# Neighbourhood attention in a transformer block: two tiles for the side transposes, other steps for the splits of the output weights, and other places for the first output sums

## The chip, the cores and the metric

The kernel runs on one core of a Trainium2 chip. The metric is the device time of one execution in microseconds (us), lower is better; a comparison uses the median of several runs. The engines are named as the profile names them: PE (TensorE, with PEld for its weight loads), DVE (VectorE), ACT (ScalarE), POOL (GpSimd) and SP (SyncE, which issues most transfers).

## The reference, cut to what matters

One layer of a trunk on 1024 latent tokens (a grid of 16 rows by 64 columns) and 256 context tokens, width 1024. The part that the change touches is the attention of 8 heads of 64 and the output projection behind it:

```python
def row_block(r):                      # one row of the grid, clamped window of 8 x 16 keys
    ...
    s_loc = jnp.einsum('bnqhd,brnkhd->bhnqrk', q_r, k_b).astype(jnp.float32) * scale
    bias = rpb[:, dr_idx[None, None, :, None], dc_idx]
    s_loc = jnp.where(col_mask, s_loc + bias.astype(jnp.float32), -jnp.inf)
    s_ctx = jnp.einsum('bnqhd,bkhd->bhnqk', q_r, k_ctx).astype(jnp.float32) * scale
    s = jnp.concatenate([s_loc.reshape(B, H, NA_NCB, NA_QB, n_loc), s_ctx], axis=-1)
    p = jax.nn.softmax(s, axis=-1).astype(v.dtype)
    o = (jnp.einsum('bhnqrk,brnkhd->bnqhd', p_loc, v_b)
         + jnp.einsum('bhnqk,bkhd->bnqhd', p_ctx, v_ctx))
...
mix_x = jnp.concatenate([_pool_mixer(u_x, pool_w[l], pool_scale[l]), attn_x], axis=-1) @ w_out[l]
x = x + gt1 * _rmsnorm(mix_x, g_post_mix[l])
```

Before it stand norm, modulation and the projections to pooling input, queries, keys and values; behind it a squared-ReLU MLP of width 4096. All arrays are float32.

## The kernel before

**Precision.** Large products are made from split operands: a high part (a rounded copy, made on ACT) and a low part (source minus high part, made on DVE), and three matmuls hi·hi, hi·lo, lo·hi (`three`, L168 to L170).

**Stages.** Projections with 8 PSUM banks in one pool up to 236 us; attention and the first two output tiles, 236 to 369 us; the remaining output tiles, norm, and the MLP in 7 products per pair of blocks (a Strassen-like scheme) up to the end.

**Attention.** A unit `(j, m)` is a pair of heads j and a band m of 8 columns of the grid, 128 tokens; there are 4 x 8 = 32 units. Bands 1 to 6 are inner (640 keys: three bands and the context), bands 0 and 7 are edge units (512 keys). The loop over `i` (36 rounds) works on four units at once, each at another stage:

- `scores(i)`: four matmuls for two heads into two tiles `S` of two banks each (L665; pool `ps_s` holds 2 of them); then on DVE one instruction for each head that adds the bias table and keeps the row minimum `nm` (L679).
- `turn(i - 2)`: PE transposes (L707) of unit i-2. The shares (one over the sums, made by `share`) and, for an inner unit, the fifth block of the probabilities go to the "sides", columns 256 to 448 of each half of the tile `pa` (1024 columns, two banks); four blocks go to two banks `T` of pool `ps_t`.
- `fifth_kept(i - 2)`: one copy on ACT (L720) takes the sides of both halves to `px` in SBUF, 2 x 192 columns for an inner unit, 2 x 64 for an edge unit.
- `exps(i, e)`: exponential on ACT (L688), one for each head. Between them `turn_kept` copies the two banks `T` to `pt` (L725), the first on ACT, the second on DVE.
- `values(i - 3)`: 20 matmuls (16 for an edge unit) into columns 0 to 256 of `pa` (L740).
- `weighed(i - 4)`: DVE multiplies the result in `pa` by the shares, into `f` (L750).

`mixed_split` splits a finished half of a head pair (`f` to `mix`) in rounds 8, 15, 16, 23, 24, 31, 32; `weight_load` and `weight_split` bring and split the first half of the output weights in the rounds that `LOADS` and `HALVES` name. Of a split, `high` (L761) issues the ACT part at once and puts off the DVE part to the next call of `low` (L762), one round later.

In the last rounds, behind the value matmuls, `out_sums` makes the first output tile in the left half of a tile `po` of pool `ps_s`; after the loop `out_kept` reads it (on ACT the sum of squares, L130; on DVE the product with the gate, L800), and then the second output tile is made in the right half of `po`. The other six tiles of that half of the columns follow as `pw` in a new pool of 8 banks.

**Order.** Instructions of PE, ACT, DVE and SP stand in the order in which the code issues them (`in_order`). The framework adds the waits: it tracks who reads and writes a tile, and accesses of two engines to one tile of PSUM wait for each other; a pool that takes over memory waits for the tiles of the pool before. SBUF pages of 1024 columns come from one pool of 33, and a new one waits for the last user of the page that it gets.

Of the kernel before, what the change touches and what calls it, by code (L numbers as in the profile page):

```python
# [10 lines left out]
F32 = mybir.dt.float32  # L11
# [6 lines left out]
P = 128  # L18
# [7 lines left out]
HD = 64  # L26
# [53 lines left out]
def hybrid_block(ctx, tc, x, ctx_in, w_mod, b_mod, gp1, gp2, w_in, pool_w, rpb, w_out, w1, w2, vectors,  # L80
                 mask, edge, out):
    nc = tc.nc
# [12 lines left out]
    def sm(name, n, bufs=1):  # L95
        return small.tile([P, n], F32, tag=name.split("_")[0], name=name, bufs=bufs)

    def page(name, dt=F32):
        return act.tile([P, 1024], dt, tag="pg", name=name)
# [29 lines left out]
    def mean_square(junk, src, ms):  # L129
        nc.scalar.activation(junk, src, AF.Square, scale=D ** -0.5, accum_out=ms)  # L130
# [32 lines left out]
    def wk(w, k, lo, c, n):  # L163
        return w[k // 2][lo][:, (k % 2) * 512 + c : (k % 2) * 512 + c + n]


    def three(ps, ahi, alo, bhi, blo, first, last, more=False):
        nc.tensor.matmul(ps, ahi, bhi, start=first, stop=False, skip_group_check=more)  # L168
        nc.tensor.matmul(ps, ahi, blo, start=False, stop=False, skip_group_check=more)  # L169
        nc.tensor.matmul(ps, alo, bhi, start=False, stop=last, skip_group_check=more)  # L170
# [46 lines left out]
    with tc.tile_pool(name="ps1", bufs=8, space=PSUM) as ps1, tc.tile_pool(name="tmp1", bufs=3) as tmp:  # L217

        def bank(name):
            return ps1.tile([P, 512], F32, tag="mm", name=name)  # L220
# [413 lines left out]
    with (  # L634
# [8 lines left out]
        units = [(j, m) for j in range(4) for m in range(NM)]  # L643
        probs, least, sums, shares, turns, turned, fifths, mixed = {}, {}, {}, {}, {}, {}, {}, {}

        pa = ps_o.tile([P, 1024], F32, tag="pa", name="pa")
        sides = pa.rearrange("p (h f) -> p h f", h=2)[:, :, 256:448]


        def scores(i):  # L650
            j, m = units[i]
            inner = 0 < m < NM - 1
            n = NKEY if inner else 4 * P
            o = 1 if m == 0 else 0
            q = qT[j][m // 4]
            cols = slice((m % 4) * P, (m % 4 + 1) * P)
            heads = [slice(e * HD, (e + 1) * HD) for e in range(2)]
            S = [ps_s.tile([P, 1024], F32, tag="S", name=f"S{j}_{m}_{e}") for e in range(2)]
            if inner:
                parts = ((128, kT[j][:, (m - 1) * P : (m + 2) * P]), (512, kc[:, j, :]))  # L660
            else:
                parts = ((0, kc[:, j, :]), (256, kT[j][:, (m + o - 1) * P : (m + o + 1) * P]))
            for c0, keys in parts:
                for e, hs in enumerate(heads):
                    nc.tensor.matmul(S[e][:, c0 : c0 + keys.shape[1]], q[hs, cols], keys[hs], start=True, stop=True)  # L665
            halves = lambda a: a.rearrange("p (a b) -> p a b", a=2)
            for e in range(2):
                t = tabs[j % 2][e]
                sp = att.tile([P, NKEY], F32, tag="sp", name=f"sp{j}_{m}_{e}", bufs=6)[:, :n]
                if inner:  # L670
                    s, bt, to = S[e][:, 128:768], t[:, :NKEY], sp
                else:
                    s, to = halves(S[e][:, 0:512]), halves(sp)
                    if o:
                        bt = halves(t[:, 2 * P : 8 * P])[:, :, P:]
                    else:
                        bt = halves(t[:, NLOC : NLOC + 512])
                nm = sm(f"nm_{i}_{e}", 1, 6)
                nc.vector.tensor_tensor_reduce(out=to, in0=s, in1=bt, scale=1.0, scalar=BIG, op0=add, op1=ALU.min,  # L679
                                               accum_out=nm)  # L680
                probs[i, e] = sp
                least[i, e] = nm
# [16 lines left out]
        def turn(i):  # L699
            inner = 0 < units[i][1] < NM - 1  # L700
            t = [bank(f"T{i}_{h}") for h in range(2)]
            turned[i] = t
            halves = [slice(h * HD, (h + 1) * HD) for h in range(2)]

            def both(to, src):
                for h, hs in enumerate(halves):
                    nc.tensor.transpose(to(h), src(hs), ident[hs, hs])  # L707

            both(lambda h: sides[:, h, :HD], lambda hs: shares[i][hs])
            for e in range(2 if inner else 0):  # L710
                both(lambda h: sides[:, h, (e + 1) * HD : (e + 2) * HD], lambda hs: probs[i, e][hs, 4 * P : 5 * P])
            for c in range(4):
                for e in range(2):
                    o = (4 * e + c) * HD
                    both(lambda h: t[h][:, o : o + HD], lambda hs: probs[i, e][hs, c * P : (c + 1) * P])

        def fifth_kept(i):
            n = (3 if 0 < units[i][1] < NM - 1 else 1) * HD
            fifths[i] = att.tile([P, 384], F32, tag="px", name=f"px{i}", bufs=4).rearrange("p (h t) -> p h t", h=2)
            nc.scalar.copy(fifths[i][:, :, :n], sides[:, :, :n])  # L720

        def turn_kept(i, h, copy):
            if h == 0:
# [29 lines left out]
        N = len(units)  # L753

        kks = (2, 3, 0, 1)
        raw_o, wo = {}, {}
        LOADS, HALVES = (9, 14, 20, 24), (13, 17, 19, 21, 25, 27, 29, 30)
        lows = []

        def high(src, hi, lo):  # L760
# [3 lines left out]
        def low():  # L764
            while lows:
                lows.pop(0)()
# [12 lines left out]
        def weight_load(h, kk):  # L779
            raw_o[h, kk] = page(f"wor{h}_{kk}")  # L780
            nc.sync.dma_start(raw_o[h, kk].rearrange("p (a f) -> p a f", a=2), pair(w_out, kk, h * 512, 512))
# [6 lines left out]
        def out_sums(ps, w, t, ns):  # L788
            b, i = t // 4, t % 4
            for n in ns:  # L790
                k, mp = order[n], mix[b][order[n]]
                three(ps, mp[:, i * P : (i + 1) * P], mp[:, 512 + i * P : 512 + (i + 1) * P],
                      wk(w, k, 0, 0, 512), wk(w, k, 1, 0, 512), n == 0, n == 7)

        def out_kept(h, t, ps, jk):
            hs = slice(h * 512, (h + 1) * 512)
            if h == 0:
                mp1[t] = page(f"mp1_{t}")
            mean_square(jk, ps, ssm[h][:, t : t + 1])
            nc.vector.tensor_tensor(mp1[t][:, hs], ps, G1[:, hs], mul)  # L800

        with in_order(ET.PE, ET.Activation, ET.DVE, ET.SP):
            for i in range(N + 4):
                if i < N and units[i][1] == 2 and units[i][0] < 3:
                    tables(units[i][0] + 1)
                if i in LOADS:
                    weight_load(0, kks[LOADS.index(i)])
                if i == N - 2:
                    G1 = gate_page("a")
                if i > 3:  # L810
                    weighed(i - 4)
                low()
                if i > 8 and i % 8 == 7:
                    mixed_split(i // 8 - 1, 1)
                if i > 0 and i % 8 == 0:
                    mixed_split(i // 8 - 1, 0)
                if i in HALVES:
                    weight_split(HALVES.index(i))
                if i < N:
                    scores(i)  # L820
                if 1 < i <= N + 1:
                    turn(i - 2)
                    fifth_kept(i - 2)
                if i < N:
                    exps(i, 0)
                if 1 < i <= N + 1:
                    turn_kept(i - 2, 0, nc.scalar.copy)
                if i < N:
                    exps(i, 1)
                if 1 < i <= N + 1:  # L830
                    turn_kept(i - 2, 1, nc.vector.tensor_copy)
                if i < 2:
                    queries(2 + i, 1, bank(f"pq{2 + i}_1"), 0)
                if 0 < i <= N:
                    share(i - 1)
                if 2 < i <= N + 2:
                    values(i - 3)

                if i == N:
                    po = ps_s.tile([P, 1024], F32, tag="S", name="po")  # L840
                if i >= N:
                    out_sums(po[:, :512], wo, 0, ((0, 1), (2, 3, 4), (5, 6, 7), ())[i - N])
            out_kept(0, 0, po[:, :512], page("jo0_0")[:, :512])
            mixed_split(3, 1)
            low()
            out_sums(po[:, 512:], wo, 1, range(8))
            out_kept(0, 1, po[:, 512:], page("jo0_1")[:, :512])

    with tc.tile_pool(name="ps2", bufs=8, space=PSUM) as ps2:

# [3 lines left out]
      with ExitStack() as tmp2:  # L854
# [323 lines left out]
        with in_order(ET.PE) as first:  # L1178
            for p in range(0, EARLY, 2):
                both = [q for q in (p, p + 1) if q < EARLY]  # L1180
# [16 lines left out]
        with tc.issue_after(first[ET.PE]), in_order(ET.PE, ET.Activation, ET.DVE, ET.SP):  # L1197
# [10 lines left out]
            def halves(name):  # L1208
                both = [page(f"{name}{i}") for i in range(2)]
                return [both[t // 2][:, (t % 2) * 512 : (t % 2) * 512 + 512] for t in range(4)]  # L1210
# [131 lines left out]
```

## Time and profile before

| | |
|---|---|
| median of 3 runs | 1073.55 us (1073.38 to 1074.51) |
| the profiled execution | 1073.15 us, its span 1071.4 us |
| busy in the span | PE 1048.6 us, DVE 686.0, ACT 504.8, POOL 55.6 |
| mean granted PE clock | 0.997 |
| attention rounds 4 to 31 (first score matmul 256.52, end of round 31 at 347.98) | 91.46 us |
| first output tile ends, second begins, third begins | 359.9, 361.52, 368.78 us |

The span is the time from the first to the last instruction of the profiled execution. In the rows of the profile a line such as `L720 ACT COPY px<-pa 128x384` gives the source line, the engine, the operation, output and input tile (buffer numbers left out), and the shape; in a timeline the first two columns are start and duration, `xN` the number of instructions merged into the row, and the bracket tells how long the engine had been idle before and what ended that. In the table of waits the columns are the total, the number and the longest wait.

### The profile page before, as it was taken

The numbers are of one execution on the slowest core, as the hardware profiler recorded it, in microseconds if no ns is written. First come the engines' busy times: TensorE is split into PE (matmuls) and PEld (weight loads), VectorE is DVE, ScalarE is ACT, GpSimd is POOL, SyncE is SP. The second block draws the span as 40 slices with busy tenths as digits, with TensorE's granted clock in tenths as the row PEclk, the third lists the DMA queues.
The fourth block names the chain that finished last, engine by engine and source line by source line (L and its number), as shares of the span: only waits on it lengthen the run. The fifth ranks groups of instructions, "written<-read, shape, count | busy, mean of one in ns | idle before, by whom it ended". The sixth has DMA issues, their size and how long they took to land.

```text
span 1071.4 us, 15228 instructions
## 1 busy us (share of the span) xinstructions
PE 1048.6 (98%) x5873; PEld 857.9 (80%) x5873; DVE 686.0 (64%) x1072; ACT 504.8 (47%) x849; POOL 55.6 (5%) x109
## 2 busy tenths in 40 slices
PE   7999999999999899999999999999999999999996
PEld 6788888867777688878888888888888888888885
DVE  5536624845899225699887667664577667556586
ACT  6553120236888123776555555454454334334441
POOL 2020000030120002200000000000000000000001
PEclk9999999999999999999999999999999999999999
DMA  9905740431010603546753535445596765546556
GB/s 341 319 21 208 246 155 0 160 109 40 22 60 30 189 1 107 170 156 196 233 201 123 191 128 166 139 144 190 194 391 231 260 240 197 197 162 212 176 185 207
DMA packets 94268, 179.37 MB, mean 167 GB/s; under 512 B 6898, under 2 KB 39154, under 8 KB 94196
## 3 DMA queue, kind: packets, MB, share of 16 engines
q1 hardware_dynamic: 76644, 144.80, 40.9%
q10 hardware_dynamic: 16272, 29.40, 7.4%
q0 software_dynamic: 1280, 4.21, 1.1%
q8 instruction: 46, 0.75, 0.3%
q14 instruction: 26, 0.21, 0.1%
HBM read 140.62 MB, written 37.76 MB: 166 GB/s over the span
## 4 chain that ended last, share of the span: by engine, by line
PE 87%; ACT 5%; DVE 4%; issue 1%; DMA 1%; POOL 1%; SPq 0%; DVEq 0%; POOLq 0%; ACTq 0%
PE pk L374 4%; PE pyv L168 3%; PE pyz L168 3%; PE pyx L169 3%; PE pyx L168 3%; PE phz L170 3%; PE phv L170 3%; PE phv L169 3%; PE phz L169 3%; PE pyv L170 3%; PE pyz L170 3%; PE pyv L169 3%; PE pyz L169 3%; PE phv L168 3%; PE phz L168 3%; PE pyx L170 3%
## 5 line engine op out<-in xcount | busy, mean ns | idle before, releaser
L992 ACT ACTIVATE c<-c 128x512 f32<-128x512 f32 x48 | 30.3, 632 | 60.4 <-DVE c L1091 23.8
L688 ACT ACTIVATE sp<-sp,nm 128x640 f32<-128x640 f32 (+1 forms) x64 | 51.4, 803 | 11.6 <-DVE nm L679 11.0
L679 DVE CUSTOM_DVE_ANT_0 sp<-S,tab 128x640 f32<-128x640 f32 (+1 forms) x56 | 42.9, 802 | 18.5 <-PE S L665 11.9
L144 DVE TENSOR_TENSOR wpS<-S,wpS 128x512 fp32r<-128x512 f32 x64 | 43.6, 686 | 12.2 <-ACT wpS L143 12.2
L168 PE MATMUL phx<-thB,wpA 128*128 128x512 f32 x128 | 50.0, 391 | 0.9 <-ACT s L1050 0.9
L170 PE MATMUL phx<-thB,wpA 128*128 128x512 f32 x128 | 49.8, 389 | 0.0
L169 PE MATMUL phx<-tlB,wpA 128*128 128x512 f32 x128 | 49.8, 389 | 0.0
L143 ACT CAST wpS<-S 128x512 fp32r<-128x512 f32 x64 | 39.1, 616 | 18.0 <-PE phy L170 7.3
L139 POOL TENSOR_TENSOR ry<-vy,nhalf 128x1 f32<-128x1 f32 x8 | 4.4, 548 | 601.9 <-DVE vy L137 601.9
L993 ACT ACTIVATE c<-c 128x512 f32<-128x512 f32 x48 | 30.3, 632 | 9.9 <-DVE sa L1063 7.7
L1099 DVE TENSOR_TENSOR c<-phz,u 128x512 f32<-128x512 f32 x16 | 11.0, 690 | 32.1 <-PE phz L170 32.1
L168 PEld LDWEIGHTS phx<-thB,wpA 128*128 128x128 f32 x128 | 24.0, 188 | 6.3 <-ACT s L1050 1.3
L665 PE MATMUL S<-kT,q 64*128 64x384 f32 (+1 forms) x128 | 28.3, 495 | 0.4 <-DVE nm L679 0.4
L800 DVE TENSOR_TENSOR mp<-pw,Ga 128x512 f32<-128x512 f32 x14 | 9.6, 688 | 29.4 <-ACT jo L130 29.4
L740 PE MATMUL pa<-pt,v 128*64 128x128 f32 x352 | 25.9, 279 | 2.3 <-ACT px L720 1.1
L170 PEld LDWEIGHTS phx<-thB,wpA 128*128 128x128 f32 x128 | 24.0, 188 | 5.1 <-DVE wpA L144 0.2
L169 PEld LDWEIGHTS phx<-tlB,wpA 128*128 128x128 f32 x128 | 24.0, 188 | 5.0
L170 PE MATMUL phv<-thT,wpS 128*128 128x512 f32 x64 | 24.9, 389 | 0.0
L168 PE MATMUL phy<-thT,wpS 128*128 128x512 f32 x64 | 24.9, 389 | 0.0
L169 PE MATMUL phy<-tlT,wpS 128*128 128x512 f32 x64 | 24.9, 389 | 0.0
L170 PE MATMUL phy<-thT,wpS 128*128 128x512 f32 x64 | 24.9, 389 | 0.0
L168 PE MATMUL phz<-thT,wpS 128*128 128x512 f32 x64 | 24.9, 389 | 0.0
(919 smaller groups left out, 3242.8 us busy)
## 6 DMA issues: line engine op xcount, KB each, us to landing
b<-in_w SPq DMA_DIRECT2D x64, 512.0 KB, 4.5
hrS<-hdS SPq DMA_DIRECT2D x32, 512.0 KB, 4.7
hrA<-hdA SPq DMA_DIRECT2D x24, 512.0 KB, 5.1
wm<-in_w_mod SPq DMA_DIRECT2D x16, 512.0 KB, 9.9
wa_0w<-in_w SPq DMA_DIRECT2D x16, 512.0 KB, 5.1
wa_1w<-in_w SPq DMA_DIRECT2D x16, 512.0 KB, 4.3
hdA<-c ACTq DMA_DIRECT2D x32, 256.0 KB, 3.4
hdS<-sa ACTq DMA_DIRECT2D x32, 256.0 KB, 4.0
```

The source lines that it names most:

```text
L143: nc.scalar.copy(hi, src)
L144: nc.vector.tensor_tensor(lo, src, hi.bitcast(F32), sub)
L168: nc.tensor.matmul(ps, ahi, bhi, start=first, stop=False, skip_group_check=more)
L169: nc.tensor.matmul(ps, ahi, blo, start=False, stop=False, skip_group_check=more)
L170: nc.tensor.matmul(ps, alo, bhi, start=False, stop=last, skip_group_check=more)
L374: nc.tensor.matmul(pks[b][j], wk(wgt, k, low, j * P, P), r, start=(k == 0 and n == 0), stop=(k == KT - 1 and n == 2))
L665: nc.tensor.matmul(S[e][:, c0 : c0 + keys.shape[1]], q[hs, cols], keys[hs], start=True, stop=True)
L679: nc.vector.tensor_tensor_reduce(out=to, in0=s, in1=bt, scale=1.0, scalar=BIG, op0=add, op1=ALU.min, accum_out=nm)
L688: nc.scalar.activation(sp, sp, AF.Exp, bias=least[i, e], scale=-1.0, accum_out=sums[i][:, e : e + 1])
L740: nc.tensor.matmul(pa[e * HD : (e + 1) * HD, cols], v[:, f : f + HD], turns[i][:, e, c] if c < 4 else fifths[i][:, :, (e + 1) * HD : (e + ...
L992: nc.scalar.activation(r, src, AF.Relu)
L993: nc.scalar.activation(r, r, AF.Square)
```

## The change

- `pa` becomes a tile of one bank (results and the sides of the first half), and the sides of the second half go to a tile `pz` of one bank of its own. `fifth_kept` issues two copies of 192 (or 64) columns in place of one that covered both.
- `LOADS` and `HALVES` name other rounds for the loads and the splits of the output weights.
- In rounds 32 to 34 the sums of the first output tile stand where the scores stood, ahead of the transposes, in place of behind the value matmuls. `po` is still a tile of `ps_s`, of which the left half is used.
- After the loop the last split of `mixed` stands ahead of `out_kept` of the first tile, and the second output tile is made in a bank `po1` of `ps_t`.

```diff
-        pa = ps_o.tile([P, 1024], F32, tag="pa", name="pa")
-        sides = pa.rearrange("p (h f) -> p h f", h=2)[:, :, 256:448]
+        pa, pz = (ps_o.tile([P, 512], F32, tag=n, name=n) for n in ("pa", "pz"))
+        sides = (pa[:, 256:448], pz[:, :192])
...
-            both(lambda h: sides[:, h, :HD], lambda hs: shares[i][hs])
+            both(lambda h: sides[h][:, :HD], lambda hs: shares[i][hs])
             for e in range(2 if inner else 0):
-                both(lambda h: sides[:, h, (e + 1) * HD : (e + 2) * HD], lambda hs: probs[i, e][hs, 4 * P : 5 * P])
+                both(lambda h: sides[h][:, (e + 1) * HD : (e + 2) * HD], lambda hs: probs[i, e][hs, 4 * P : 5 * P])
...
-            nc.scalar.copy(fifths[i][:, :, :n], sides[:, :, :n])
+            for h in range(2):
+                nc.scalar.copy(fifths[i][:, h, :n], sides[h][:, :n])
...
-        LOADS, HALVES = (9, 14, 20, 24), (13, 17, 19, 21, 25, 27, 29, 30)
+        LOADS, HALVES = (8, 10, 17, 19), (12, 13, 14, 20, 21, 22, 28, 30)
...
                 if i < N:
                     scores(i)
+                else:
+
+                    if i == N:
+                        po = ps_s.tile([P, 1024], F32, tag="S", name="po")[:, :512]
+                    out_sums(po, wo, 0, ((0, 1), (2, 3, 4), (5, 6, 7), ())[i - N])
                 if 1 < i <= N + 1:
                     turn(i - 2)
                     fifth_kept(i - 2)
...
                 if 2 < i <= N + 2:
                     values(i - 3)
-
-                if i == N:
-                    po = ps_s.tile([P, 1024], F32, tag="S", name="po")
-                if i >= N:
-                    out_sums(po[:, :512], wo, 0, ((0, 1), (2, 3, 4), (5, 6, 7), ())[i - N])
-            out_kept(0, 0, po[:, :512], page("jo0_0")[:, :512])
             mixed_split(3, 1)
             low()
-            out_sums(po[:, 512:], wo, 1, range(8))
-            out_kept(0, 1, po[:, 512:], page("jo0_1")[:, :512])
+            out_kept(0, 0, po, page("jo0_0")[:, :512])
+            po = bank("po1")
+            out_sums(po, wo, 1, range(8))
+            out_kept(0, 1, po, page("jo0_1")[:, :512])
```

## The prediction

> **What bounds the kernel now.** I read the page first: the span, the busy time of each engine, and the shares of the chain that ended last.
>
> ```profile
> span 1071.4 us, 15228 instructions
> ...
> PE 1048.6 (98%) x5873; PEld 857.9 (80%) x5873; DVE 686.0 (64%) x1072; ACT 504.8 (47%) x849; POOL 55.6 (5%) x109
> ...
> PE 87%; ACT 5%; DVE 4%; issue 1%; DMA 1%; POOL 1%; SPq 0%; DVEq 0%; POOLq 0%; ACTq 0%
> ```
>
> TensorE (PE) is busy for 98% of the span and carries 87% of the chain. So a microsecond comes off only where PE stands still, and the edit touches one stage, attention and the first output tiles (236 to 369 us). Its waits come second (columns: total us, times, longest):
>
> ```profile
> PEld pa L740 <- ACT px L720: 6.6, 24, 0.5
> ...
> PE pa L740 <- ACT px L720: 1.9, 6, 0.4
> ...
> PEld pa L707 <- DVE f L750: 1.5, 5, 0.7
> ```
>
> In 24 of the 32 rounds the value matmuls (L740) wait for ACT's copy of the side transposes (L720). I call round i "step i", from its first score matmul (L665) to the next round's. Steps 4 to 6 last 3.35, 3.34 and 3.34. The timeline of step 6, an inner one:
>
> ```profile
> 264.39 0.22 PE L707 MATMUL pa<-ident,rb 64*128 64x64 f32 x2
> ...
> 264.57 0.66 PE L707 MATMUL T<-ident,sp 64*128 64x64 f32 x16
> ...
> 264.78 0.48 ACT L720 COPY px<-pa 128x384 f32<-128x384 f32 x1 [0.39 <-PE pa L707]
> 265.31 0.64 PEld L740 LDWEIGHTS pa<-pt,v 128*64 128x64 f32 x12 [0.21 <-ACT px L720]
> 265.31 0.88 PE L740 MATMUL pa<-pt,v 128*64 128x128 f32 x12
> ...
> 265.51 0.83 ACT L688 ACTIVATE sp<-sp,nm 128x640 f32<-128x640 f32 x1 [0.26 <-DVE nm L679]
> ```
>
> The transposes into T start at 264.57 and the values at 265.31, 0.74 later, 0.05 after the copy ended; the copy started after the last side transpose. Step 9 turns an edge unit, whose copy has 128 elements:
>
> ```profile
> 274.04 0.67 PE L707 MATMUL T<-ident,sp 64*128 64x64 f32 x16
> ...
> 274.27 0.27 ACT L720 COPY px<-pa 128x128 f32<-128x128 f32 x1 [0.63 <-PE pa L707]
> ...
> 274.64 0.88 PE L740 MATMUL pa<-pt,v 128*64 128x128 f32 x12
> ```
>
> Here the same distance is 0.60, with no wait. So the copy costs an inner step 0.14. The timeline of the end, third:
>
> ```profile
> 359.63 0.39 PE L170 MATMUL po<-wo_3h,mix 128*128 128x512 f32 x1
> 360.06 0.60 ACT L130 ACTIVATE jo<-po 128x512 f32<-128x512 f32 x1 [6.23 <-PE po L170]
> ...
> 360.77 0.69 DVE L800 TENSOR_TENSOR mp<-po,Ga 128x512 f32<-128x512 f32 x1 [2.69 <-ACT jo L130]
> ...
> 361.52 0.50 PE L168 MATMUL po<-wo_2h,mix 128*128 128x512 f32 x1 [1.50 <-DVE mp L800]
> ...
> 368.03 0.69 DVE L800 TENSOR_TENSOR mp<-po,Ga 128x512 f32<-128x512 f32 x1 [5.96 <-ACT jo L130]
> ...
> 368.78 0.50 PE L168 MATMUL pw<-wo_2h,mix 128*128 128x512 f32 x1 [1.50 <-DVE mp L800]
> ```
>
> The second output tile (361.52) waits for square and product of the first, which lies in the other half of the same tile `po`; PE stands for 1.5 us, and again for 1.5 us before `pw` at 368.78. After that PE waits for other engines once for 0.9 us and once for 0.2 us, so what is saved here reaches the end. The built order shows that everything from `pw` on is the same in both programs, waits included.
>
> **The change, part by part.** The sum is made against the profiled execution: 1073.15 us (span 1071.4 and 1.75 around it), 0.40 below the median 1073.55. Pieces of a step without waits, from the rows above and their like: scores to sides 1.18 (0.97 for an edge unit), sides to T 0.18 (0.055 edge), T to values 0.60, values to next scores 1.24 (1.03 edge). An inner step is then 3.20, steps 7 and 8 are 2.99, step 9 is 3.075, step 10 2.865.
>
> *Two copies.* In the built program the values wait for the copy out of `pa` alone, now 192 elements. No row shows 192: 128 take 0.265, 384 take 0.474, and the line between gives 0.317, which I take as the row of 128 is near; the ends stay for the range. Started after the fifth side transpose (0.03 sooner), it ends 0.68 after the sides began, and the weights of the values could load at 0.71 anyway: the wait is gone. The second copy costs ACT about 0.07 to 0.15 more per step. Cover for it: ACT stands 0.26 before the exponential at 265.51, waiting for DVE. Without that cover the exponentials move back by as much, and the next value matmuls with them only in steps that also split.
>
> *Steps that split.* Where ACT's queue holds a weight or `mixed` split (0.51 before the copy), the values start 5.46 after the scores of the step before: 294.19 against 288.73, 320.50 against 315.04, 346.73 against 341.27, the same chain of exponentials, split, copy each time. A copy 0.16 shorter makes that 5.30, so with 1.24 two steps take at least 6.54, against 6.40 for PE. DVE in such a step: two score reductions 0.75 each, copy 0.60, shares and weighing 0.53, low part 0.61, so 3.24; also close to 3.27.
>
> *Splits moved.* Before, splits at 17, 19 and 25, 27 follow the edge units, where PE steps are short: DVE lags (its reduction of step 18 starts 1.62 after the scores, 1.38 elsewhere) and steps 19 and 27 take 3.82 and 3.77. Step 11 has the same units without a weight split: 3.29. After, no weight split stands in 15 to 19 or 23 to 27, only those of `mixed`; so 19 and 27 become a step 11, less 0.14: 3.15. The new runs, 12 to 16, 20 to 24 and 28 to 31, go by the 6.54 of ACT. The loads go from steps 9, 14, 20, 24 to 8, 10, 17, 19; on SP's queue the third is moved past the tables' rows of step 18. They land 3.7 us after issue, and SP runs some steps ahead. The one now ahead of the rows waits for a page that step 14 frees; the rows were issued at 293.27, in step 15, land 3.7 later, POOL's 12 operations of 0.47 take 5.6, and step 24 starts at 321.7: 19 us of slack. Nothing; without it DVE would wait in step 24.
>
> Sum of the steps. 3 to 8 and 11: seven waits of 0.13 to 0.15, 0.98. 12 to 16: 16.53 now; after, 3.52 (the scores of step 11 lag 0.13, so 6.67 - 3.15), 3.20, 3.34 and 3.20 (pairs of 6.54), 2.99, so 16.25; 20 to 24: likewise 16.53 to 16.25; 28 to 31: 13.41 to 13.26; together 0.71. 17 to 19: 9.78 to 9.09 (3.075 + 2.865 + 3.15), 25 to 27: 9.70 to 9.09; together 1.30. Stage: 2.99.
>
> *The end.* From the last values of step 31 (347.98) to the second output tile now: 0.53 to the sides (0.46 waiting for DVE's `f`), 0.23, 0.86 (waiting for the copy), 1.25, 1.58 for two sums, 0.11, 0.59, 1.25, 2.27 for three, 1.03, 3.84 for three and the wait: 13.5. After, the sums come first in each round and cover `f` and the copy: 1.58 + 0.20 + 0.60 + 1.25 + 2.27 + 0.11 + 0.59 + 1.25 + 2.27 + 1.03 = 11.15. `po1` waits only for PE itself. Square and product of `po` now stand behind the split of `mixed` on ACT and DVE (0.6 and 0.7), all under the 5.5 us of `po1`'s matmuls; without them 1.5 would be back. The second stall stays: in the built program `pw` waits for the product that reads `po1`, though that is another bank; 1.5, counted at nothing. Gain 2.37.
>
> Total 2.99 + 2.37 = 5.36: 1073.15 to 1067.8 for the profiled execution, 1068.2 for the median.
>
> [...] Rows: exponentials and copies on ACT start about 0.1 before the one ahead has ended (the split at 286.45 lasts 0.61, the copy behind it starts at 286.96), so part of an instruction's fixed cost is hidden. [...]
>
> **The rivals.**
> 1. *The shorter copy buys little.* If 192 elements take nearly the 0.47 of 384, the wait stays, and ACT pays two. For it: no row of 192; against: 128 take 0.265. Left are the 2.37 of the end and steps 19 and 27 at some 3.3, 1.0: gain 3.4, 1070.2.
> 2. *Every wait of the stage goes*, those of ACT's chain and of scores on DVE too: steps 4 to 31 then take 86.1 against 91.5, so 5.4 with 2.4 at the end and 0.1 in step 3: 7.9, 1065.6. Against: 5.30 in the splitting steps.
> 3. *Slower: DVE and ACT lag in the runs of splits.* In steps 12 to 16, 20 to 24, 28 to 31 ACT (3.27), DVE (3.24) and PE (3.20) are within 2%; a lag of one passes to the next, as in steps 19 and 27 now, which lost 0.5 each. At 0.5 above their present times in 14 steps it loses 7.0, against 0.98 + 1.30 + 2.37 = 4.65 elsewhere: 1075.9. From 0.33 a step the sign turns. For it: the two steps of now; against: those followed short PE steps, while in the runs PE needs 3.20 itself.
> 4. *The same lag at half strength*, 0.25 a step: 1072.4, not to be told from now.
>
> **How the numbers follow.** Forecast 0.62 (gain 4.2 to 6.6), rival 1 0.15, rival 2 0.08, rival 4 0.09, rival 3 0.06. Time 1068.2. The range runs from 1066.0, with most of rival 2's way towards it, to 1071.4, which takes in rival 1 with its copy at the upper bound and more lag; rivals 3 and 4 and the far end of 2 are left out. A measurement of this kernel tells about 0.2% (2.1 us) from nothing: faster 0.85, within it 0.09, slower 0.06.
>
> **What would show it.** Copies of 192 near 0.32 us; T to values at 0.60 in steps 4 to 8; steps 19 and 27 near 3.15; pairs of splitting steps at 6.5; no PE stall between the end of `po` and `po1`; a stall of 1.5 before `pw`. The forecast is wrong if splitting steps stay at 3.35 or above (copy or lag), if `pw` starts without its stall (1.5 more gain), or if the time after `pw` is not the same as now.

## The result and the profile after

The changed kernel took 1068.24 us (median of 4 runs, 1067.96 to 1068.45) against 1073.57 us (4 runs, 1073.38 to 1074.51) of the kernel before: a ratio of 0.9948, with a 95% interval of 0.9935 to 0.996. The forecast was 1068.2. The profiled execution took 1068.25 us.

The page of the changed kernel, the same three lines:

```profile
span 1066.5 us, 15252 instructions
...
PE 1047.9 (98%) x5873; PEld 859.5 (81%) x5873; DVE 686.2 (64%) x1072; ACT 507.0 (48%) x881; POOL 55.6 (5%) x109
...
PE 89%; ACT 4%; DVE 3%; issue 1%; DMA 1%; POOL 1%; SPq 0%; DVEq 0%; POOLq 0%; ACTq 0%
```

The span is 4.9 us shorter, TensorE (PE) is as busy as before (1047.9 us against 1048.6), and ACT has 32 instructions and 2.2 us more, the second copies. So what went is time in which PE stood still. The waits between 236 and 369 us (columns: total us, times, longest):

```profile
PEld pa L741 <- ACT px L721: 2.6, 9, 0.6
...
PEld pa L707 <- DVE f L751: 0.8, 4, 0.2
...
PE pa L741 <- ACT px L721: 0.6, 2, 0.4
```

Value matmuls wait for a copy 9 times instead of 24. Step 6, the inner step shown before, in the timeline of the changed kernel:

```profile
264.59 0.67 PE L707 MATMUL T<-ident,sp 64*128 64x64 f32 x16
...
264.78 0.32 ACT L721 COPY px<-pa 128x192 f32<-128x192 f32 x1 [0.24 <-PE pz L707]
265.00 0.33 ACT L721 COPY px<-pz 128x192 f32<-128x192 f32 x1
265.18 0.64 PEld L741 LDWEIGHTS pa<-pt,v 128*64 128x64 f32 x12
265.18 0.88 PE L741 MATMUL pa<-pt,v 128*64 128x128 f32 x12
...
265.53 0.83 ACT L688 ACTIVATE sp<-sp,nm 128x640 f32<-128x640 f32 x1 [0.21 <-DVE nm L679]
```

The transposes into T start at 264.59 and the values at 265.18, 0.59 later, with no wait. The first copy (192 elements) takes 0.32 and ends at 265.10; the second starts 0.22 after the first. The exponential behind them still stands 0.21, waiting for DVE: the second copy lies in time that ACT did not use.

The end of the stage, same timeline, further on:

```profile
355.18 0.40 PE L170 MATMUL po<-wo_3h,mix 128*128 128x512 f32 x1
...
356.53 0.50 PE L168 MATMUL po<-wo_2h,mix 128*128 128x512 f32 x1
...
357.57 0.59 ACT L130 ACTIVATE jo<-po 128x512 f32<-128x512 f32 x1
...
358.31 0.68 DVE L801 TENSOR_TENSOR mp<-po,Ga 128x512 f32<-128x512 f32 x1
...
363.83 0.50 PE L168 MATMUL pw<-wo_2h,mix 128*128 128x512 f32 x1 [1.56 <-DVE mp L801]
```

The second output tile starts at 356.53, ahead of the square (357.57) and the product (358.31) of the first; the stall ahead of it is gone. The stall before `pw` (363.83) is still there, 1.56.

In the tables, "stage" is the time from the first score matmul of step 0 to the end of step 31, "end" the time from there to the first matmul of `pw`.

| steps | before | forecast | after | copies only | splits only | high parts behind |
|---|---|---|---|---|---|---|
| 3 to 8, 11 | 23.43 | 22.45 | 22.46 | 22.77 | 23.58 | 22.46 |
| 12 to 16 | 16.53 | 16.25 | 16.43 | 16.06 | 16.58 | 15.74 |
| 17 to 19 | 9.78 | 9.09 | 9.07 | 9.86 | 9.22 | 9.07 |
| 20 to 24 | 16.53 | 16.25 | 16.15 | 16.07 | 16.71 | 15.66 |
| 25 to 27 | 9.70 | 9.09 | 9.08 | 9.54 | 9.22 | 9.07 |
| 28 to 31 | 13.41 | 13.26 | 13.13 | 13.08 | 13.45 | 12.92 |
| stage | 111.24 | 108.25 | 108.22 | 109.28 | 110.67 | 106.83 |
| end | 20.80 | 18.43 | 18.47 | 20.85 | 20.84 | 18.48 |

(The forecast column is the column before less the gains that the prediction gives.) After `pw` the two programs take 702.6 us each. So the 5.36 us between the first scores and `pw` is the whole gain: 3.02 from the stage, 2.33 from the end (the span shows 0.4 less, since the first scores start at 237.14 instead of 236.73; in the profiles of this case that start lies between 236.5 and 237.7).

### The profile page after: what moved, and what is told of

Its sections match the earlier page's. It is cut to its first block, busy times and chain, and to the rows that moved or that the text cites. A ratio compares the mean times of both kernels' runs of the same rounds, so it can differ in the third digit from the quotient of the medians.

```text
span 1066.5 us, 15252 instructions
## 1 busy us (share of the span) xinstructions
PE 1047.9 (98%) x5873; PEld 859.5 (81%) x5873; DVE 686.2 (64%) x1072; ACT 507.0 (48%) x881; POOL 55.6 (5%) x109
## 4 chain that ended last, share of the span: by engine, by line
PE 89%; ACT 4%; DVE 3%; issue 1%; DMA 1%; POOL 1%; SPq 0%; DVEq 0%; POOLq 0%; ACTq 0%
PE pk L374 4%; PE S L665 3%; PE pa L741 3%; PE pyx L168 3%; PE pyv L168 3%; PE pyz L168 3%; PE pyx L169 3%; PE phv L170 3%; PE phv L169 3%; PE phz L169 3%; PE phz L170 3%; PE pyv L170 3%; PE pyz L170 3%; PE pyv L169 3%; PE pyz L169 3%; PE phz L168 3%
## 5 line engine op out<-in xcount | busy, mean ns | idle before, releaser
L169 PE MATMUL phv<-tlT,wpS 128*128 128x512 f32 x64 | 24.9, 389 | 0.0
L168 PE MATMUL phz<-thB,wpS 128*128 128x512 f32 x64 | 24.9, 389 | 0.0
L169 PE MATMUL phz<-tlT,wpS 128*128 128x512 f32 x64 | 24.9, 389 | 0.0
L168 PE MATMUL phv<-thT,wpA 128*128 128x512 f32 x64 | 24.9, 389 | 0.0
L170 PE MATMUL phv<-thT,wpA 128*128 128x512 f32 x64 | 24.9, 389 | 0.0
```

## The experiments

Each ratio below is to the kernel before, run in alternation on the same chip: 1074.33 us for the first four kernels (32 runs), 1073.83 us for the last four (15 runs). Where two kernels differ by a microsecond or less, I go by their profiles, by the same stretches. Each profile is one execution, and the runs of one kernel spread over 0.2 to 2.9 us.

### One part at a time

The first kernel has only the two tiles and the two copies:

```diff
-        pa = ps_o.tile([P, 1024], F32, tag="pa", name="pa")
-        sides = pa.rearrange("p (h f) -> p h f", h=2)[:, :, 256:448]
+        pa, pz = (ps_o.tile([P, 512], F32, tag=n, name=n) for n in ("pa", "pz"))
+        sides = (pa[:, 256:448], pz[:, :192])
...
-            nc.scalar.copy(fifths[i][:, :, :n], sides[:, :, :n])
+            for h in range(2):
+                nc.scalar.copy(fifths[i][:, h, :n], sides[h][:, :n])
```

> Of the change only the two tiles pa and pz with two copies; splits and end as before. The theory by steps: the values wait for the copy of 192 alone, so transposes into T to values falls from 0.74 to 0.60 in the 14 or so waiting steps that do not split, little in steps that split after one that does not, 0.16 in steps 19 and 27, and 0.16 in round 32: about 2.9 us less than the kernel before. The rival that the copies are hidden and the whole gain is the end and the moved splits: within 0.5 us of before.

Measured: 1071.77 us (10 runs), 0.9976 [0.9967, 0.9985]. The stage is 1.96 shorter. T to values is 0.59 to 0.60 in the inner steps that do not split, and those steps take 3.20. In 12 to 15, 20 to 23 and 28 to 31 steps of 3.20 and of 3.34 alternate in this kernel, and each pair takes 6.54, the figure that the prediction has for a pair on ACT's chain. Steps 19 and 27 fall only to 3.67 and 3.61, since their splits are still there, and step 18 takes 3.12 where it took 2.88. One step misses altogether: 7 took 3.31, where 2.99 was due and the changed kernel took 3.02. Two timelines show why, the first of this kernel, the second of the changed one (`rb` is the copy of the shares that `share` makes, `tab` a bias table that POOL makes):

```profile
266.81 1.26 POOL L605 TENSOR_TENSOR tab<-msk,U 128x128 f32<-128x128 f32 x3 [31.09 <-DVE ri L692]
266.83 0.51 DVE L694 COPY rb<-ri 128x128 f32<-128x128 f32 x1
...
267.59 0.14 PEld L707 LDWEIGHTS pa<-ident,rb 64*128 64x128 f32 x1 [0.50 <-DVE f L751]
```

```profile
266.89 0.23 DVE L694 COPY rb<-ri 128x128 f32<-128x128 f32 x1
266.91 1.33 POOL L605 TENSOR_TENSOR tab<-msk,U 128x128 f32<-128x128 f32 x3 [31.12 <-DVE ri L692]
...
267.37 0.14 PEld L707 LDWEIGHTS pa<-ident,rb 64*128 64x128 f32 x1 [0.21 <-DVE f L751]
```

Where DVE's copy starts 0.02 after POOL's first operation, it takes 0.51 instead of 0.23, DVE's `f` comes later, and the side transposes wait 0.50 for it; where it starts 0.02 ahead, nothing is lost. Two other kernels below show the long copy (0.49 in both) and the long step (3.28 in both). In the profiles of the kernel before and of the changed one the copies of this line that start outside an operation of POOL take 0.23, and those that take longer (0.30 at 302.23 in the first, 0.41 at 298.13 and 0.24 at 301.61 in the second) all start inside one and end 0.08 after it. So the odd step 7 is a matter of a few hundredths of a microsecond between DVE and POOL, and no part of the change.

The second kernel has only the new places of loads and splits:

```diff
-        LOADS, HALVES = (9, 14, 20, 24), (13, 17, 19, 21, 25, 27, 29, 30)
+        LOADS, HALVES = (8, 10, 17, 19), (12, 13, 14, 20, 21, 22, 28, 30)
```

> Of the change only the new rounds for loads and splits. The theory by steps: steps 19 and 27 fall from 3.82 and 3.77 to about 3.29, all others stay: 1.0 us less than before. The rival that runs of splits make DVE and ACT lag: steps 12 to 16 and 20 to 24 grow past 3.36 and the time is the same or above.

Measured: 1073.16 us (11 runs), 0.9991 [0.9982, 1.0], hardly to be told from none by the time alone. In the profile steps 19 and 27 take 3.15 and 3.29 instead of 3.82 and 3.77, which is 1.15 of gain, and 0.6 is given back: 12 and 28 take 3.41 each, 20 takes 3.55, 18 takes 3.00 and step 7 the 3.28 of the long copy on DVE. The later steps of the runs take 3.34 to 3.36 each, what they took before. So two or three splits in a row build up no lag, even with the long copy. That speaks against the mechanism of rivals 3 and 4.

The third kernel has only the end:

```diff
+                else:
+                    if i == N:
+                        po = ps_s.tile([P, 1024], F32, tag="S", name="po")[:, :512]
+                    out_sums(po, wo, 0, ((0, 1), (2, 3, 4), (5, 6, 7), ())[i - N])
...
-                if i == N:
-                    po = ps_s.tile([P, 1024], F32, tag="S", name="po")
-                if i >= N:
-                    out_sums(po[:, :512], wo, 0, ((0, 1), (2, 3, 4), (5, 6, 7), ())[i - N])
...
+            po = bank("po1")
```

> Of the change only the end: sums ahead of the transposes in the last rounds, po1 in its own bank, the last split of mixed ahead of the first tile's square. The theory: from the end of round 31 to the second output tile 11.2 us instead of 13.5, the 1.5 us before pw stay: 2.3 us less than before. The rival that both stalls go: 3.9 less; that the sums only move the waits: under 1.

Measured: 1071.81 us (11 runs), 0.9975 [0.9967, 0.9984]. The second output tile starts 11.33 after the end of step 31 and `pw` 18.64 after it, against 20.80 before: a gain of 2.16, with its stall of 1.56 in place.

From the first scores to `pw` the three parts alone gain 1.92, 0.54 and 2.03, together 4.49; the whole change gains 5.36. By the medians they gain 2.56, 1.17 and 2.52, together 6.25, more than the 5.33 of the whole change; so each part's share of the time is known to about half a microsecond; which steps belong to which part is read from the profiles. Of the 0.87 that the profiles leave, 0.44 is the odd step 7 (0.29 in the first kernel, 0.15 in the second). Another 0.21 is in steps 17 to 19 and 25 to 27: the copies alone gain 0.08 there and the splits alone 1.04, the whole change 1.33.

### The order of the two copies

If the gain came from ACT's instructions being shorter, it would not matter which half is copied first. If it came from the values waiting for the copy out of `pa` alone, it would:

```diff
-            for h in range(2):
+            for h in (1, 0):
                 nc.scalar.copy(fifths[i][:, h, :n], sides[h][:, :n])
```

> The changed kernel with the two copies in the other order, pz first. The theory: the values wait for the copy out of pa, which now ends some 0.22 later than in the changed kernel and 0.03 later than the one copy of before; transposes into T to values goes to about 0.77, and the gain of the copies is lost: about 2.5 to 3.5 us above the changed kernel, some 2.5 below before. The rival that shorter ACT instructions as such help: like the changed kernel within 0.5.

Measured: 1072.32 us (11 runs), 0.998 [0.9971, 0.9989]. The stage takes 111.50, 3.28 more than in the changed kernel, and steps 4 to 6 take 3.40 each. The timeline of step 6 in this kernel:

```profile
264.58 0.67 PE L707 MATMUL T<-ident,sp 64*128 64x64 f32 x16
...
264.79 0.32 ACT L721 COPY px<-pz 128x192 f32<-128x192 f32 x1 [0.45 <-PE pz L707]
265.00 0.32 ACT L721 COPY px<-pa 128x192 f32<-128x192 f32 x1
...
265.38 0.64 PEld L741 LDWEIGHTS pa<-pt,v 128*64 128x64 f32 x12 [0.27 <-ACT px L721]
```

The copy out of `pa` is now the second; it ends at 265.32, and the values start 0.06 later. Their weights stood 0.27 for it. T to values is 0.80, more than the 0.74 of one long copy, though each copy takes the same 0.32. So the gain lies in which copy the values wait for. Two copies as such cost: from the start of the first to the end of the second is 0.53, against 0.48 for the one of 384, and with the wrong order that stands on the path.

### The second output tile in the same two banks as the first

```diff
-                        po = ps_s.tile([P, 1024], F32, tag="S", name="po")[:, :512]
-                    out_sums(po, wo, 0, ((0, 1), (2, 3, 4), (5, 6, 7), ())[i - N])
+                        po = ps_s.tile([P, 1024], F32, tag="S", name="po")
+                    out_sums(po[:, :512], wo, 0, ((0, 1), (2, 3, 4), (5, 6, 7), ())[i - N])
...
-            po = bank("po1")
-            out_sums(po, wo, 1, range(8))
+            out_sums(po[:, 512:], wo, 1, range(8))
```

> The changed kernel with the second output tile back in the right half of po. The theory: its matmuls wait again for square and product of the first tile, which now also stand behind the last split of mixed on ACT and DVE: 2.0 to 2.5 us above the changed kernel, all of it between the last values and the second tile. The rival that the place does not matter because the halves are different banks: no difference.

Measured: 1072.29 us (11 runs), 0.9985 [0.9976, 0.9994]; the changed kernel had 0.9948, so this costs some 4 us. The stall came as worked out, 2.44: on ACT and DVE the split of `mixed` now stands ahead of square and product. But `pw` starts 8.84 after the second tile's first matmul, not 7.30. The timeline and the same stretch in windows (the column ahead of the last two is the granted clock) tell why:

```profile
358.98 0.63 PE L168 MATMUL po<-wo_2h,mix 128*128 128x512 f32 x1 [2.44 <-DVE mp L801]
...
359.41 0.63 PE L169 MATMUL po<-wo_2l,mix 128*128 128x512 f32 x1
...
362.39 0.50 PE L170 MATMUL po<-wo_3h,mix 128*128 128x512 f32 x1
...
362.74 0.39 PE L168 MATMUL po<-wo_0h,mix 128*128 128x512 f32 x1
...
367.82 0.50 PE L168 MATMUL pw<-wo_2h,mix 128*128 128x512 f32 x1 [1.50 <-DVE mp L801]
```

```profile
core 0: us, PE busy (x) PEld busy (x) DVE busy (x) ACT busy (x) POOL busy (x), PEclk, DMA share, GB/s
358.50:359.00 0.50, 0.02 (x1) 0.02 (x1) 0.43 (x1) 0.00 (x0) 0.00 (x0) 1.00 1.01 270
359.00:359.50 0.50, 0.50 (x2) 0.40 (x3) 0.00 (x0) 0.00 (x0) 0.00 (x0) 0.70 0.99 221
359.50:360.00 0.50, 0.50 (x3) 0.40 (x2) 0.00 (x0) 0.00 (x0) 0.00 (x0) 0.50 1.05 262
362.00:362.50 0.50, 0.50 (x3) 0.40 (x2) 0.00 (x0) 0.00 (x0) 0.00 (x0) 0.50 1.15 262
362.50:363.00 0.50, 0.50 (x4) 0.42 (x3) 0.00 (x0) 0.00 (x0) 0.00 (x0) 0.88 0.94 221
363.00:363.50 0.50, 0.50 (x4) 0.41 (x3) 0.00 (x0) 0.00 (x0) 0.00 (x0) 1.00 1.10 262
```

The 3.42 us ahead of the drop, same columns:

```profile
355.78:359.20 3.42, 0.98 (x15) 0.74 (x12) 1.58 (x3) 1.21 (x3) 0.00 (x0) 1.00 1.02 242
```

The matmuls behind the stall take 0.63 us instead of 0.39, and start 0.43 apart instead of 0.23. The granted clock is 0.50 for 3.4 us: by the shares of the windows at its two ends (0.70 and 0.88) from 359.20 to 362.62. Of that, 1.6 us is lost: `pw` starts 1.54 later behind the second tile's first matmul than in the changed kernel, though its own stall is 0.06 shorter. In the 3.42 us ahead of the drop PE worked for 0.98 us and stood for 2.44. The stalls of 1.50 us in the kernel before and of 1.56 in the changed one left the granted clock at 1.00; how long a stall has to be for the drop is not shown. Of the 11 runs two took 1070.5 us, about the changed kernel's time and the stall alone (1068.24 + 2.44 = 1070.7); that these two kept their clock is my estimate from that sum and not shown, as they have no profile: their mean granted clock is 0.997, that of the other nine 0.993 to 0.997.

### The high parts behind the copies

In the changed kernel values still wait 9 times, all of them in steps where a split's high part stands ahead of the copies on ACT. The next kernel moves both kinds of split behind the copies in ACT's order:

```diff
-                if i > 8 and i % 8 == 7:
-                    mixed_split(i // 8 - 1, 1)
-                if i > 0 and i % 8 == 0:
-                    mixed_split(i // 8 - 1, 0)
-                if i in HALVES:
-                    weight_split(HALVES.index(i))
...
                     fifth_kept(i - 2)
+                if i > 8 and i % 8 == 7:
+                    mixed_split(i // 8 - 1, 1)
+                if i > 0 and i % 8 == 0:
+                    mixed_split(i // 8 - 1, 0)
+                if i in HALVES:
+                    weight_split(HALVES.index(i))
```

> The changed kernel with the high parts of the splits issued behind the two copies in ACT's order, not ahead of them. The theory: the 5.30 chain of splitting steps goes, the values start 0.60 after the transposes into T in all steps, and ACT has room (its work in such a step is some 3.1 us): steps 12 to 16, 20 to 24 and 28 to 31 fall towards PE's own 3.20 and 2.99: 0.6 to 1.1 us below the changed kernel. The rival that ACT or DVE is the bound there anyway (the exponentials start 0.25 later): no gain, or up to 1 us of loss.

Measured: 1067.32 us (5 runs), 0.9942 [0.993, 0.9955]. That is 0.92 below the changed kernel, within what was expected; the stage is 106.83, 1.39 less. The rest does not reach the time: 2.14 us of this execution lie outside its span, where the changed kernel has 1.77. The profile does not show what fills them. Two timelines of the same step, the changed kernel's first:

```profile
289.33 0.61 ACT L762 CAST wo_3h<-wor 128x512 fp32r<-128x512 f32 x1
...
289.47 0.66 PE L707 MATMUL T<-ident,sp 64*128 64x64 f32 x16
...
289.83 0.31 ACT L721 COPY px<-pa 128x192 f32<-128x192 f32 x1
290.05 0.32 ACT L721 COPY px<-pz 128x192 f32<-128x192 f32 x1
290.20 0.63 PEld L741 LDWEIGHTS pa<-pt,v 128*64 128x64 f32 x12 [0.21 <-ACT px L721]
...
290.71 0.83 ACT L688 ACTIVATE sp<-sp,nm 128x640 f32<-128x640 f32 x1 [0.34 <-ACT px L721]
```

```profile
289.34 0.67 PE L707 MATMUL T<-ident,sp 64*128 64x64 f32 x16
...
289.53 0.32 ACT L721 COPY px<-pa 128x192 f32<-128x192 f32 x1
289.75 0.33 ACT L721 COPY px<-pz 128x192 f32<-128x192 f32 x1
289.93 0.64 PEld L741 LDWEIGHTS pa<-pt,v 128*64 128x64 f32 x12
...
289.96 0.63 ACT L762 CAST wo_3h<-wor 128x512 fp32r<-128x512 f32 x1
...
290.60 0.83 ACT L688 ACTIVATE sp<-sp,nm 128x640 f32<-128x640 f32 x1
```

In the changed kernel the first copy starts 0.36 after T, behind the split, and the values 0.73 after T. With the split behind the copies, the first copy starts 0.19 after T and the values 0.59, without a wait. The exponential then starts 0.67 after the values, where it was 0.35 in the inner step 6; that delay does not reach PE, as this step takes 3.20. No wait of the values for a copy is left in this kernel, and steps 12 to 15, 20 to 23 and 28 to 30 take 3.06 to 3.21 instead of 3.20 to 3.50 (31 alone grew, from 3.20 to 3.32).

### Where the new pool takes its memory

```diff
-    with (
+    ps_t = ctx.enter_context(tc.tile_pool(name="ps_t", bufs=2, space=PSUM))
+    ps_o = ctx.enter_context(tc.tile_pool(name="ps_o", bufs=1, space=PSUM))
+    with (
         tc.tile_pool(name="ps_s", bufs=2, space=PSUM) as ps_s,
-        tc.tile_pool(name="ps_t", bufs=2, space=PSUM) as ps_t,
-        tc.tile_pool(name="ps_o", bufs=1, space=PSUM) as ps_o,
...
-    with tc.tile_pool(name="ps2", bufs=8, space=PSUM) as ps2:
+    with tc.tile_pool(name="ps2", bufs=4, space=PSUM) as ps2:
+      places = [(ps2, "mm")] * 4 + [(ps_t, "T")] * 2 + [(ps_o, "pa"), (ps_o, "pz")]
```

The banks are then given out in turn over `places`: `pw` comes from a pool that takes over the memory of the score tiles alone, and the other two pools stay open.

> The changed kernel with the pools arranged so that pw takes only the memory of the score tiles, and so waits for the product of po, not of po1. The theory: pw starts 5.7 us after po1 in place of 7.3, all behind it unchanged: 1.5 to 1.6 us below the changed kernel. The rival that the stall only moves to the next tile or into the later stage: the same time as the changed kernel.

Measured: 1066.46 us (5 runs), 0.9933 [0.9919, 0.9947]. The timeline at the change of tiles:

```profile
361.90 0.39 PE L170 MATMUL po<-wo_3h,mix 128*128 128x512 f32 x1
...
362.13 0.39 PE L168 MATMUL pw<-wo_2h,mix 128*128 128x512 f32 x1
...
362.39 0.60 ACT L130 ACTIVATE jo<-po 128x512 f32<-128x512 f32 x1 [4.12 <-PE po L170]
```

`pw` starts 0.23 after the matmul ahead of it, with no wait, and 5.58 after the second tile's first (356.55). The end takes 16.75 instead of 18.47, and everything behind `pw` still 702.5 us, so the stall has not moved there. (The stage of this profile is 108.67, 0.45 more than in the changed kernel; it has the long copy on DVE in steps 7 and 18.) So the 1.5 us before `pw` were not a need of the data: the first tile of a new pool waited for the last reader in a closed pool's memory, though that reader worked in another bank.

The last kernel has both edits:

> Splits behind the copies and the pools together. The theory: the two gains add, 2.1 to 2.7 us below the changed kernel.

Measured: 1065.23 us (5 runs, 1064.92 to 1066.36), 0.9923 [0.9911, 0.9936], the fastest of all. Stage 106.83, end 16.76: the two gains add, 3.1 us in the profile and 3.0 in the medians (2.7 by the two ratios), at the upper end of what was expected or above it.

## Why the prediction was right

**The sum.** Forecast: 2.99 from the stage, 2.37 from the end, total 5.36. Measured: 3.02, 2.33 and, from the first scores to `pw`, 5.36. The medians give 5.33.

**Two copies.** A copy of 192 takes 0.316 us out of `pa` (mean of the 24 inner rounds), 0.317 was interpolated. T to values went from 0.74 to 0.59 or 0.60, and 3 to 8 with 11 gained 0.97 of the 0.98 forecast. The second copy costs ACT 2.2 us over 32 rounds, 0.07 a step, the lower of the two bounds. Its cover was rightly named: ACT's idle time before the exponential fell from 0.26 to 0.21 in step 6.

**Steps that split.** The values of step 14 start 5.30 after the scores of step 13 (290.20 against 284.90), as worked out. Within the runs the sizes were off both ways. Steps 12, 20 and 28 took 3.40, 3.40 and 3.39, where the sum has 3.52: the lag of the scores at the edge unit was carried over in full, and 0.12 of it did not arrive. Step 15 took 3.50 instead of 3.20. There the exponential ahead of it starts at 290.71, 0.34 after the copy ended, though its input from DVE was there at 290.34; the line names the copy as the releaser. The same 0.3 is in three profiles in which ACT has the same instructions in the same order (this one, the one with a single `po`, the one with other pools), and not in those with the split moved. What ACT waited for is open. The two errors, 0.37 in all and 0.30, nearly cancel: 0.76 for the three runs, where 0.71 was forecast. That the sum came out so close here is luck. The prediction named splitting steps of 3.35 or above as a sign of error; four of them are (12, 15, 20 and 28), but its own sum had three at 3.52, and only step 15 was not foreseen.

**Splits moved.** Steps 19 and 27 took 3.14 and 3.15, forecast 3.15; 17 to 19 and 25 to 27 gained 1.33 of 1.30. The kernel with the splits alone shows the same steps at 3.15 and 3.29, so this gain is the splits' own. The loads cost nothing, as counted.

**The end.** The second tile starts 11.17 after step 31, forecast 11.15. The prediction said that `po1` waits only for PE itself, and put a stall of 1.5 on the case that square and product were not covered. The kernel with a single `po` shows the cause is right and the price too low: 2.44, as square and product now stand behind a split, and some 1.6 more where the granted clock was 0.50. The stall before `pw` stayed at 1.56, as counted.

**The overlap of the copies.** In step 6 the second copy starts 0.22 after the first, 0.10 before that one has ended, so the two take 0.53 of ACT from start to end, where the one copy took 0.48. The steps that split gained 0.76 with it.

**The rivals.** Rival 1 (the copy stays long) falls by the 0.316. Rivals 3 and 4 (a lag through the runs of splits) fall by the kernel with the splits alone: the first step of a run took 0.07 to 0.21 more there, the others nothing. Rival 2 (every wait goes) did not happen, as nine waits in splitting steps stayed; the kernel with the high parts behind the copies removed those nine and took 87.13 for steps 4 to 31, where that rival has 86.1 and the changed kernel 88.54. So the chain of exponential, split and copy did hold these steps, and it was an order on ACT, not its load.

**Expectations that missed.** The copies alone were expected to bring 2.9 and the splits alone 1.0. By the medians they came near (2.56 and 1.17); by the profiles they brought 1.92 and 0.54, with the odd step 7 in both, and with steps left long that only the other part shortens. The kernel with a single `po` was expected 2.0 to 2.5 above the changed kernel and is some 4 above it; the 3.4 us at a granted clock of 0.50 behind the stall had not been counted. The split moved behind the copies brought 1.39 in the stage, where 0.6 to 1.1 was expected, since it also removed the stand of 0.3 in step 15.

## What to carry to other kernels

Ask of a copy that feeds a matmul which part of it the matmul needs first; give that part its own tile and put it first on its engine, and put work that nothing waits for soon behind it: the order on ACT, which is busy for 71% of the time from 236 to 369 us, gained 1.4 us of the stage here, and the wrong order lost 3.3. The two waits of PE for an instruction in another bank (1.50 us each in the kernel before) were bookkeeping of a tile and of a pool here, and went when the tile and the pool were cut along the banks. A stall of PE cost more than its length here: the one of 2.44 us lost another 1.6 us behind it, at a granted clock of 0.50. And before an odd step is put down to the change, compare the lengths of the instructions ahead of it on the engine that it waits for: here 0.3 us of a step was a copy on DVE that started inside an operation of POOL and took 0.51 us in place of 0.23.

## What was not expected of the hardware

A stall of PE of 2.44 us, with 0.98 us of work in the 3.4 us up to the drop, was followed by 3.4 us at a granted clock of 0.50, and so cost 1.6 us more than itself (the kernel with a single `po`). Behind the stalls of 1.50 us in the kernel before and of 1.56 us in the changed one the granted clock was 1.00.

DVE's copy `rb` (0.23 us) took 0.30 in the kernel before, 0.41 in the changed one and 0.51 in the one with the copies alone, where it started inside an operation of POOL on the tables; the first two ended 0.08 after that operation.

One reading is open: the 0.3 us that ACT stands before the exponential ahead of step 15. No wait in the trace explains it. An 8 KB transfer of instructions starts 1.6 to 1.7 us behind it in all three profiles, but the two kernels with the split moved have one at nearly the same time (292.21 and 291.86) and ACT does not stand there; no run was made on it.
